# Splitting each layer's token tile into halves, with the second half's input projections placed beside (mLSTM/HGRN) or behind (SSD) the chunk recurrences of the first

## The chip, the cores and the metric

The kernel runs on all 8 cores of one Trainium2 chip. Every core executes the same program on its own share of the batch. The metric is the device time of the slowest core, in microseconds (us).

A program on 8 cores shows two states here. In the slow one the cores of one die, or of both, are granted a lower TensorE clock, and the time is some per cent longer (in one run of the kernel before, the cores of one die took 11202 to 11253 us at a clock of 0.723 to 0.729, those of the other 11531 to 11618 us at 0.688 to 0.695). Each execution is marked fast or slow by its cores' spans and clocks. Engines are named PE (TensorE matmul), PEld (TensorE weight load), DVE (VectorE), ACT (ScalarE), POOL and SP.

## The reference, cut to what matters

The program is one inference step of a two-layer trunk. One combined input projection feeds three head groups, each a recurrence over chunks of frames; an output projection and a feed-forward block (FFN) follow.

```python
def trunk_layer(x, state, p):
    h = rmsnorm(x, p['norm_mix'])
    proj = jnp.einsum('btd,dc->btc', h, p['w_in'])          # 1024 -> 6680 columns
    (z, xbc, dt_raw, mq, mk, mv, mi, mf, mo, hq, hf, hi, hgate) = split_cols(proj, IN_SIZES)
    conv = p['conv_b'] + sum(xpad[:, w:w + t] * p['conv_w'][w] for w in range(CONV_W))   # 4 taps, causal
    xbc = silu(conv)
    h_fin, y = lax.scan(ssd_chunk, h0, ssd_in)              # recurrence 1: SSD
    ...                                                     # gated by silu(z), rmsnorm
    (mc, mn, mm), hc = lax.scan(mlstm_chunk, carry0, ml_in) # recurrence 2: mLSTM
    y_ml = sigmoid(mo) * hc
    fgate = lb + (1 - lb) * sigmoid(hf)
    s_fin, o = lax.scan(gla_chunk, hg_st, hg_in)            # recurrence 3: HGRN2, log(fgate), silu(hq)
    y_hg = o * silu(hgate)
    x = x + einsum(concat([y_ssd, y_ml, y_hg]), p['w_out'])
    return x + swiglu_ffn(rmsnorm(x))                       # and the new states
```

The batch is 16 prompt streams of 2048 frames and 32 running streams of 32 frames. A core has 2 prompt streams, cut into tiles of 512 frames, and one sample tile of 4 streams of 32 frames. So it goes through 16 prompt layers (8 tiles, 2 layers) and 2 sample layers.

## The kernel before

The kernel records every operation with the keys it reads and writes, and a scheduler puts in the semaphores. Each engine's operations stand in its queue in the order in which the code commits them, and the trace shows PE taking its matmuls in that order: below, a projection that needs nothing from the chunks starts only 0.38 us after the start of their last matmul. A fence is one small DVE operation that comes after all work recorded before it and before all work recorded later. A prompt layer works through four chunks of 128 frames, in this order (cuts marked with dots):

```python
def layer(l, tile):
    ...
    fence_all()
    rmsnorm_fm(...)
    wvz, wkeyz = wload(w_in_v[:, :, 0:1024], 8, 1024, ...)       # a 2 MB slice of w_in
    ...
    def conv_chunk(b, cc):                  # one block of 128 channels, 512 frames
        ...
        V("act", copy(xp3[:, :, 3:3 + ls], PS[b][:, 0:n]))       # PSUM -> xp, ONE buffer
        ...
        V("dve", tensor_scalar(acc3, xp3[:, :, 0:ls], ...))      # tap 0, ONE accumulator cacc
        for w in range(1, 4):
            V("dve", scalar_tensor_tensor(acc3, xp3[:, :, w:w + ls], ...))
        V("act", activation(xbcT[:, cc, 0:n], cacc[:, 0:n], AF.Silu))
    for cc in range(12):
        b = fm_proj(wv, wkey, cc * 128, 128, n, hT, "hT", 8)     # 8 matmuls of 512 columns
        conv_chunk(b, cc)                                        # with z evictions in between
    ...
    pipelined([S.capture(one_chunk, l, tile, ci, ch, "ssd", ssd_chunk) for ci, ch in enumerate(chunks)], l)

    fence_all()
    ...                                                          # q, k, v, i, f: 512 columns each
    for ci, ... in enumerate(chunks):
        V("act", activation(oTM[...], PS[b], AF.Sigmoid))
    for hh in range(4):
        V("act", activation(gqT[:, hh, 0:n], PS[b], AF.Silu))
    for hh in range(4):                                          # the HGRN gate
        V("act", activation(cacc, PS[b], AF.Sigmoid))
        V("dve", tensor_scalar(cacc, cacc, oml, lb, ALU.mult, ALU.add))
        V("act", activation(gT[:, hh, 0:n], cacc, AF.Ln))
    ...
    for ci, ch in enumerate(chunks):                             # a "pair": same 128 frames
        la = S.capture(one_chunk, l, tile, ci, ch, "ml", mlstm_chunk)
        lb = S.capture(one_chunk, l, tile, ci, ch, "hg", hgrn_chunk)
        interleave2(la, lb)
```

`pipelined` puts the part of chunk c+1 that needs no carried state between the operations of chunk c. `interleave2(a, b)` cuts two lists of operations at their matmuls and deals them into the queues in turn. In the chunk loops two streams use four of the eight PSUM banks each.

## Time and profile before

| | before |
|---|---|
| time, median of the first 6 executions | 11292.55 us (11228.0 to 11406.7) |
| time, median of 20, beside the changed kernel | 11367.15 us (11228.0 to 11625.88) |

These lines of the page give the span, busy time by engine (share of the span, instructions), the DMA total and the chain of waits that ended last.

```profile
span 11256.1 us, 108345 instructions; the slowest of 8 cores (11192.9 to 11256.1 us)
PE 6586.1 (59%) x33519; PEld 3287.3 (29%) x33519; DVE 4136.5 (37%) x8286; ACT 3364.1 (30%) x6579; POOL 13.8 (0%) x37
...
DMA packets 596050, 766.59 MB, mean 68 GB/s; under 512 B 8884, under 2 KB 400332, under 8 KB 593160
...
PE 46%; DVE 18%; ACT 13%; issue 10%; DMA 8%; another core or an unknown queue 4%; DVEq 1%; ACTq 0%; SPq 0%
```

No engine is near full: PE 59%, DVE 37%, ACT 30%. The chain goes back and forth between engines, so the limits have to be looked for stage by stage. The windows view below shows one prompt layer, cut where its parts start. Columns: the stretch, its length, busy time and instruction count of PE, PEld, DVE, ACT and POOL, the granted clock, the DMA share and the rate. The rows are: norm, conv and SSD projections; SSD chunks; mLSTM/HGRN projections; pair one; pair two; pairs three and four with the output projection; FFN.

```profile
core 1: us, PE busy (x) PEld busy (x) DVE busy (x) ACT busy (x) POOL busy (x), PEclk, DMA share, GB/s
4828.13:4912.82 84.69, 44.72 (x176) 18.35 (x176) 42.31 (x83) 28.34 (x40) 0.00 (x0) 0.78 0.18 63
4912.82:5034.14 121.32, 69.72 (x364) 37.59 (x364) 62.64 (x94) 43.53 (x96) 0.00 (x0) 0.50 0.00 1
5034.14:5114.03 79.89, 67.21 (x296) 29.29 (x297) 6.48 (x20) 32.44 (x44) 0.00 (x0) 0.90 0.33 112
5114.03:5151.79 37.76, 12.33 (x81) 7.53 (x79) 21.93 (x53) 22.26 (x48) 0.00 (x0) 0.56 0.00 1
5151.79:5183.58 31.79, 10.38 (x72) 6.82 (x72) 21.82 (x53) 14.06 (x36) 0.00 (x0) 0.50 0.00 0
5183.58:5291.83 108.25, 50.83 (x273) 26.70 (x273) 49.94 (x116) 28.04 (x72) 0.00 (x0) 0.62 0.19 64
5291.83:5428.75 136.92, 121.64 (x548) 54.20 (x548) 28.60 (x44) 19.26 (x26) 1.47 (x5) 0.95 0.36 112
```

The first row is 84.69 us with PE busy for 44.72: not PE-bound. Its cause shows in the timeline of one conv block (start, length, engine, operation, what it waited for):

```profile
4864.30 0.72 ACT L143 ACTIVATE arenaB<-arenaB,arenaA 128x512 bf16<-128x512 f32 x1 [3.32 <-DVE arenaB L143]
...
4864.93 0.58 ACT L143 ACTIVATE arenaB<-ps 128x512 bf16<-128x512 f32 x1
4865.41 0.57 ACT L143 COPY arenaB<-ps 128x512 f32<-128x512 f32 x1
...
4866.16 0.48 DVE L143 TENSOR_SCALAR arenaB<-arenaB,arenaA 128x512 f32<-128x512 f32 x1
4866.75 2.46 DVE L143 SCALAR_TENSOR_TENSOR arenaB<-arenaB,arenaA 128x512 f32<-128x512 f32 x3
4869.30 0.72 ACT L143 ACTIVATE arenaB<-arenaB,arenaA 128x512 bf16<-128x512 f32 x1 [3.32 <-DVE arenaB L143]
```

The blocks follow each other every 5.0 us (4864.30 to 4869.30): Silu of the last block, a z eviction (the Silu that takes a block of z out of PSUM, the buffers that matmuls write), the copy into `xp`, four taps on DVE, Silu. With one `xp` and one `cacc` this is a single chain, and PE does not set its pace: it is busy through all of this block and for 0.48 us of the 5.0 us from 4874.30, where it waits for a weight load, and the chain's next round takes 5.06 us all the same (Silu at 4874.36 and at 4879.42).

The second row is a chain of latencies too (clock 0.50, nobody over 60% busy). In the third row PE is busy for 67.21 of 79.89 us at clock 0.90: after a wait of 10 us for the first weights, this one is PE's. Pairs run at clock 0.50 to 0.56 with PE busy for a third: here there is room for PE work, which is what the change aims at.

One line of the groups (count, busy us, mean ns):

```profile
L143 ACT ACT_TABLE_LOAD x291 | 373.4, 1283 | 642.1 <-PE ps L143 331.0
```

ACT loads a function table 291 times at 1283 ns.

To compare kernels, I took from the trace's start times the same marks in all 16 prompt layers and give medians: start of the layer, first scan (TENSOR_TENSOR_SCAN on DVE) of the SSD chunks, the state's cast in each of them, the second fence, the first scan of each pair, the third fence. All "steps" and "stages" below are worked out in this way, on the slowest core unless said otherwise.

### The profile page before, as it was taken

What the parts mean: (1) busy time and instruction counts of PE and PEld (TensorE: products, weight loads), DVE (VectorE), ACT (ScalarE), POOL (GpSimd) and SP (SyncE); (2) the same over time, 40 slices, a digit from 0 to 9 for tenths busy, and PEclk for the clock granted to TensorE, in tenths of its full rate; (3) what the DMA queues carried; (4) which work ended last, traced back from release to release, by engine and by line L of the source; (5) the groups of instructions that cost most, each with busy time, mean ns of one, the idle gap of its engine ahead of it and who ended that gap; (6) DMA issues with size and microseconds to landing.
All of it is one profiled execution on the core that took longest, in us unless ns stands there. A gap on an engine that the chain in (4) does not pass through costs nothing.

```text
span 11256.1 us, 108345 instructions; the slowest of 8 cores (11192.9 to 11256.1 us)
## 1 busy us (share of the span) xinstructions
PE 6586.1 (59%) x33519; PEld 3287.3 (29%) x33519; DVE 4136.5 (37%) x8286; ACT 3364.1 (30%) x6579; POOL 13.8 (0%) x37
## 2 busy tenths in 40 slices
PE   0046757575757566565657565757575665655444
PEld 0012323232323232222323232323232322223333
DVE  0033343434243433443343434342434334433333
ACT  0024242414242423323242424242424233231323
POOL 0000000000000000000000000000000000000000
PEclk9957767686868676767767676868686767676666
DMA  9941212121212121111212131212121211112323
GB/s 109 114 66 57 70 49 92 34 92 34 98 43 77 49 74 55 62 49 66 77 49 77 42 99 34 92 34 95 46 77 49 75 53 64 48 66 70 107 67 113
DMA packets 596050, 766.59 MB, mean 68 GB/s; under 512 B 8884, under 2 KB 400332, under 8 KB 593160
## 3 DMA queue, kind: packets, MB, share of 16 engines
q1 hardware_dynamic: 593032, 689.31, 18.7%
q0 software_dynamic: 2464, 70.35, 5.6%
q8 instruction: 291, 4.77, 0.2%
q14 instruction: 263, 2.15, 0.1%
HBM read 799.86 MB, written 100.48 MB: 80 GB/s over the span
## 4 chain that ended last, share of the span: by engine, by line
PE 46%; DVE 18%; ACT 13%; issue 10%; DMA 8%; another core or an unknown queue 4%; DVEq 1%; ACTq 0%; SPq 0%
PE ps L143 46%; DVE arenaB L143 15%; ACT arenaB L143 9%; DVE arenaA L143 3%; DMA arenaA<-w_in_b 2%; ACT arenaA L143 2%; ACT L143 1%; DMA arenaB<-x_prompt 1%; DVEq L139 1%; DMA arenaA<-w_ffn_out_b 1%; DMA arenaA<-w_out_b 0%; DMA arenaA<-w_ffn_in_b 0%; ACTq L139 0%; DMA arenaA<-conv_b 0%
## 5 line engine op out<-in xcount | busy, mean ns | idle before, releaser
L143 PE MATMUL ps<-arenaA 128*128 128x512 bf16 (+7 forms) x18051 | 4034.3, 385 | 1214.8 <-DMA arenaA<-norm_ffn 304.2
L143 PEld LDWEIGHTS ps<-arenaA 128*128 128x128 bf16 (+6 forms) x18051 | 1799.7, 104 | 3569.1 <-issue 1935.8
L143 PE MATMUL ps<-arenaA,arenaB 128*128 128x128 f32 (+14 forms) x4836 | 1156.9, 373 | 2156.3 <-ACT arenaB L143 945.7
L143 DVE TENSOR_TENSOR arenaB<-arenaB 128x512 f32<-128x512 f32 (+17 forms) x2184 | 1367.2, 643 | 913.6 <-ACT arenaB L143 825.7
L143 PE MATMUL ps<-arenaB,arenaA 128*128 128x512 bf16 (+6 forms) x6696 | 1225.3, 347 | 505.1 <-DVE arenaB L143 258.1
L143 PEld LDWEIGHTS ps<-arenaA,arenaB 128*128 128x128 f32 (+11 forms) x4836 | 592.8, 161 | 2376.8 <-issue 2359.6
L143 ACT ACTIVATE arenaB<-ps 128x512 bf16<-128x512 f32 (+6 forms) x1476 | 784.4, 532 | 1371.2 <-PE ps L143 1252.5
L143 ACT ACTIVATE arenaB<-arenaB 128x512 f32<-128x512 f32 (+15 forms) x1668 | 748.7, 454 | 1285.5 <-DVE arenaB L143 1233.4
L143 PEld LDWEIGHTS ps<-arenaB,arenaA 128*128 128x128 bf16 (+5 forms) x6696 | 685.0, 125 | 1088.7 <-issue 779.9
L143 PE MATMUL ps<-arenaB 128*128 128x64 bf16 (+8 forms) x3936 | 492.3, 264 | 788.3 <-DVE arenaB L143 648.7
L143 DVE TENSOR_TENSOR arenaA<-arenaA,ps 128x512 f32<-128x512 f32 (+2 forms) x648 | 394.6, 609 | 1410.0 <-PE ps L143 1396.4
L143 ACT ACTIVATE arenaB<-arenaA 128x4096 bf16<-128x4096 f32 (+1 forms) x45 | 149.9, 3332 | 2321.0 <-DVE arenaA L143 2321.0
L143 DVE TENSOR_TENSOR arenaB<-arenaB,ps 128x512 bf16<-128x512 bf16 (+5 forms) x684 | 414.1, 605 | 1153.6 <-PE ps L143 1114.0
L143 ACT ACT_TABLE_LOAD x291 | 373.4, 1283 | 642.1 <-PE ps L143 331.0
L143 PEld LDWEIGHTS ps<-arenaB 128*128 128x128 bf16 (+3 forms) x3936 | 292.5, 123 | 928.5 <-issue 916.9
L143 ACT ACTIVATE arenaA<-ps,arenaA 128x128 bf16<-128x128 f32 (+1 forms) x1152 | 414.2, 360 | 316.5 <-PE ps L143 233.3
L143 DVE SCALAR_TENSOR_TENSOR arenaB<-arenaB,arenaA 128x512 f32<-128x512 f32 (+1 forms) x648 | 457.9, 707 | 69.3 <-DVE arenaB L143 2.3
L143 ACT COPY arenaB<-ps 128x512 f32<-128x512 f32 (+9 forms) x648 | 359.6, 563 | 410.0 <-PE ps L143 393.4
L143 ACT ACTIVATE arenaB<-arenaB,arenaA 128x512 bf16<-128x512 f32 (+3 forms) x360 | 197.4, 548 | 868.9 <-DVE arenaB L143 862.2
L143 DVE SCALAR_TENSOR_TENSOR arenaA<-arenaA 128x512 bf16<-128x512 f32 (+3 forms) x360 | 254.4, 707 | 433.4 <-ACT arenaA L143 399.5
L143 DVE TENSOR_SCALAR arenaB<-arenaB,arenaA 128x512 f32<-128x512 f32 (+2 forms) x306 | 144.7, 473 | 529.6 <-ACT arenaB L143 529.4
L143 DVE COPY arenaA<-ps 128x512 f32<-128x512 f32 (+4 forms) x99 | 59.7, 603 | 618.6 <-PE ps L143 608.4
(37 smaller groups left out, 1702.5 us busy)
## 6 DMA issues: line engine op xcount, KB each, us to landing
arenaA<-w_in_b SPq DMA_DIRECT2D x90, 2048.0 KB
arenaA<-w_ffn_in_b SPq DMA_DIRECT2D x90, 2048.0 KB
arenaA<-w_ffn_out_b SPq DMA_DIRECT2D x72, 1408.0 KB
arenaA<-w_out_b SPq DMA_DIRECT2D x36, 2048.0 KB
w_in_b<-w_in POOLq DMA_DIRECT2D x2, 13360.0 KB, 290.9
w_ffn_in_b<-w_ffn_in POOLq DMA_DIRECT2D x2, 11264.0 KB, 435.9
arenaA<-w_in_b SPq DMA_DIRECT2D x18, 1056.0 KB
arenaA<-w_in_b SPq DMA_DIRECT2D x18, 1040.0 KB
```

What stands on the lines that cost most here:

```text
L139: eng.wait_ge(sem, val)
L143: ins = getattr(eng, name)(*a, **k)
```

## The change: intent and diff

The intent: cut each layer's tile in two halves of two chunks; run the projections of the second half on idle PE time while the chunk recurrences of the first half go on. It does so for both parts of the layer, but a switch (`DBGSEQ=True`) makes the SSD part sequential. For this the PSUM banks are divided into three, three and two, and the body of the SSD chunk takes its banks one group at a time.

```diff
-            i = 4 * p + (psk[p] % 4)
+            if p == 2:                       # the projections of the second half
+                i = 6 + (psk[2] % 2)
+                psk[2] += 1
+                return i
+            i = 3 * p + (psk[p] % 3)
...
+            hsplit = (len(allc) + 1) // 2 if len(allc) >= 2 else len(allc)
+            for part in (allc[:hsplit], allc[hsplit:]):
+                ...                          # t0, nt: first frame and length of the half
-            b = fm_proj(wv, wkey, cc * 128, 128, n, hT, "hT", 8)
+            def proj_ssd(sub):               # the same code for one half: weights loaded again,
+                ...                          # 256 columns, conv in two pieces
+                    b = fm_proj(wv, wkey, cc * 128, 128, nt, hT, "hT", 8, t0)
+            def proj_mlhg(sub):
+                ...
-            pipelined([S.capture(...) for ci, ch in enumerate(chunks)], l)
+            proj_ssd(subs[0])
+            for k, sub in enumerate(subs):
+                lists = [S.capture(one_chunk, l, tile, ci, ch, "ssd", ssd_chunk) for ci, ch in sub["chunks"]]
+                Y = S.capture(pipelined, lists, l)
+                if k + 1 < len(subs):
+                    X = cap_pool2(proj_ssd, subs[k + 1])
+                    if DBGSEQ:
+                        commit_all(Y)
+                        commit_all(X)
+                    else:
+                        interleave2(Y, X)
+                else:
+                    commit_all(Y)
...
+            proj_mlhg(subs[0])
+            for k, sub in enumerate(subs):
+                ...                          # Y: the pairs of this half, each interleaved as before
+                if k + 1 < len(subs):
+                    X = cap_pool2(proj_mlhg, subs[k + 1])
+                    interleave2(Y, X)
```

The sample tile is cut in the same way (its four streams of 32 frames become two and two).

## The prediction

> **What bounds the kernel now.** No single engine: busy times (page part 1) are PE 59%, DVE 37%, ACT 30%; the chain of waits runs 46% through PE, 18% DVE, 13% ACT. A prompt layer takes about 590 us; I cut one (timeline, 4832 to 5428 us) into stages with the windows view:
> - SSD projections and conv, 4845 to 4909: serial ACT-DVE-ACT chain, 5.03 us per 128-channel block with a z eviction, 4.55 us without; PE is not the limit.
> - SSD chunks, 4909 to 5034: PE 54% busy, DVE 51%, ACT 36%, clock 0.50. A latency chain: prologue 16.6 us, then 28.1 us per chunk, last body 18 us.
> - mLSTM/HGRN projections, 5044 to 5121: PE 69 of the first 72 us, clock 0.96.
> - mLSTM/HGRN chunks, 5121 to 5250: about 31.8 us per pair, DVE 60%, ACT 43%, PE 29%, clock 0.51.
> - output projection and FFN: PE-bound; untouched.
>
> **What the change does.** It hides half of the third stage in the first half of the fourth, where PE idles. In the SSD part it hides nothing: the switch is left at sequential, so second-half projections queue behind the first two chunks on every engine.
>
> **Costs per prompt layer** (estimates from trace durations):
> 1. Conv twice at 256 columns. The sample tile at 128 columns takes 3.0/2.5 us per block; interpolating, 3.67/3.2 at 256, so 40 us per half, 80 against 58: +22.
> 2. SSD pipeline broken in two: 2 x (16.6+28.1+18) against 16.6+3x28.1+18: +6.5. Handover +1.
> 3. Three PSUM banks instead of four per stream: +2 to +5.
> 4. First-half mLSTM/HGRN projections: PE 36 us, but 8.2 MB of weights are loaded again per half, and a 2 MB load takes about 9.6 us (issue 5076.9, PE resumes 5086.5), so DMA stretches it; with ACT's gate chain about 50, against 77: -27.
> 5. First two pairs, now with the second half's projections: 64 us alone. In-order queues insert 28 matmul groups, 28 evictions and some 20 extra table loads of 1.28 us (Sigmoid and Silu alternate with Exp; 13 today, all outside the chunk loop). Only two banks serve them. [...] I expect 105: +41.
> 6. Last two pairs unchanged.
>
> Sum about +45 per layer at worst; with a better overlap in 5 (85 us) +25. I take +35: 16 x 35 + 2 x 30 for the sample tile = +620, shaded to +590. Items 1, 2, 4, 5 lie on the critical path. W_in traffic doubles (+246 MB), mostly hidden.
>
> **Predicted:** 11880 us, range 11520 to 12260. Chances: faster by over 2% 0.06, within 2% 0.11, slower by over 2% 0.83.
>
> **What would show it.** DMA bytes about 1010 MB; table loads up from 291 to 600-800; conv period 3.2 to 3.7 us with PE idle; a second prologue in each SSD stage; no projection matmul before the last matmul of the first two SSD chunks; pairs one and two 45 to 60 us each, three and four about 32; FFN the same 118 us.
>
> **What would make it wrong.** [...] the inserted work fits the gaps (pairs near 40 us): about 11600. Key-level dependences and two banks serialise the streams: over 12200. If the SSD half had been interleaved after all, item 2 would turn to a gain.

No term of the sum is cut: +22, +6.5 and +1, +2 to +5, -27 and +41 make 45.5 to 48.5, recorded as about +45. The +41 was the author's estimate: the trace has a granted clock of 0.51 in the pairs against 0.96 in the dense projections, and the inserted matmuls might cost near double.

## The result, and the profile after

| | before | after |
|---|---|---|
| median | 11367.15 us (20 executions) | 12202.7 us (10 executions, 12102.09 to 12340.9) |
| ratio of fast runs | | 1.0766, 95% interval 1.0711 to 1.0822: slower |

A ratio is the mean time of one kernel's fast runs over that of the other's of the same rounds, so it is not quite the ratio of the medians above. The outputs are correct. The prediction had the class right, and 12202.7 lies within its range, but near its upper end.

The page of the changed kernel, the same lines as before:

```profile
span 12244.3 us, 124454 instructions; the slowest of 8 cores (12201.4 to 12244.3 us)
PE 7028.5 (57%) x37983; PEld 3783.5 (31%) x37983; DVE 4407.9 (36%) x9762; ACT 3971.1 (32%) x7821; POOL 13.8 (0%) x37
...
DMA packets 745896, 1013.88 MB, mean 83 GB/s; under 512 B 11188, under 2 KB 457932, under 8 KB 742920
...
PE 43%; DVE 18%; ACT 15%; issue 11%; DMA 8%; another core or an unknown queue 3%; DVEq 1%; ACTq 0%; SPq 0%
...
L146 ACT ACT_TABLE_LOAD x651 | 835.2, 1283 | 839.1 <-PE ps L146 491.7
```

The span of the profiled execution grew by 988 us (11256.1 to 12244.3). PE, DVE and ACT work grew by 442, 271 and 607 us. ACT's share of the chain rose from 13% to 15% and the waits for DMA stayed at 8%. Two predicted marks are there: 1013.88 MB against about 1010, and 651 table loads against 600 to 800.

The same layer in windows. The rows: norm and first-half conv; first two SSD chunks; second-half conv; last two SSD chunks; first-half mLSTM/HGRN projections; pair one; pair two; pairs three and four with the output projection; FFN.

```profile
core 7: us, PE busy (x) PEld busy (x) DVE busy (x) ACT busy (x) POOL busy (x), PEclk, DMA share, GB/s
5259.83:5324.10 64.27, 24.23 (x144) 14.69 (x144) 30.87 (x84) 20.84 (x36) 0.00 (x0) 0.72 0.42 148
5324.10:5387.40 63.30, 33.77 (x178) 18.34 (x179) 30.04 (x45) 20.94 (x45) 0.00 (x0) 0.50 0.00 1
5387.40:5434.80 47.40, 25.82 (x137) 14.51 (x135) 25.50 (x74) 15.81 (x35) 0.00 (x0) 0.72 0.07 23
5434.80:5502.45 67.65, 36.13 (x186) 19.80 (x186) 32.06 (x48) 22.04 (x48) 0.00 (x0) 0.50 0.00 1
5502.45:5561.94 59.49, 38.14 (x235) 23.96 (x236) 5.14 (x17) 24.03 (x38) 0.00 (x0) 0.82 0.61 204
5561.94:5603.00 41.06, 28.39 (x188) 17.02 (x186) 22.46 (x56) 26.43 (x60) 0.00 (x0) 0.80 0.22 75
5603.00:5659.56 56.56, 29.97 (x170) 17.42 (x168) 24.16 (x61) 42.10 (x70) 0.00 (x0) 0.64 0.11 40
5659.56:5768.81 109.25, 51.90 (x278) 26.78 (x276) 49.94 (x115) 30.00 (x74) 0.00 (x0) 0.64 0.19 63
5768.81:5906.75 137.94, 121.51 (x548) 54.11 (x548) 28.59 (x43) 19.27 (x26) 1.47 (x5) 0.95 0.35 111
```

Compare with before. Conv and projections of the SSD part took 84.69 us and now take 64.27 and 47.40. The chunks took 121.32 and now take 63.30 and 67.65. The mLSTM/HGRN projections fell from 79.89 to 59.49, pair one rose from 37.76 to 41.06, pair two from 31.79 to 56.56. The rest, with the FFN, is about the same here. In medians over all 16 prompt layers:

| step, us | before | after |
|---|---|---|
| layer start to first SSD scan | 84.7 | 63.7 |
| first scan to first chunk's state cast | 16.8 | 17.6 |
| chunk 1 to 2 | 28.2 | 28.4 |
| chunk 2 to 3 | 28.1 | 81.9 |
| chunk 3 to 4 | 28.2 | 28.4 |
| chunk 4 to fence | 17.4 | 18.6 |
| fence to pair one (projections) | 67.6 | 48.5 |
| pair one | 38.2 | 42.1 |
| pair two | 32.0 | 56.2 |
| pair three | 32.0 | 33.1 |
| **SSD stage** | **203.5** | **239.0** |
| **mLSTM/HGRN stage, with output projection** | **231.5** | **244.2** |
| **FFN stage** | **135.3** | **137.8** |

Adding the profiled layers up (sums, not medians): the SSD stages of the prompt layers grew by 565 us, the mLSTM/HGRN stages by 179, the two sample layers by 142 in all, and the FFN by 104. These make 990 of the 988 us.

The 104 us of the FFN come with a lower granted clock and not with more work; whether the change provokes that clock is left open. Two FFN stages of the changed kernel, of equal instruction counts in PE:

```profile
3781.90:3935.50 153.60, 138.91 (x536) 57.42 (x536) 26.66 (x41) 19.27 (x26) 0.00 (x0) 0.83 0.35 113
6424.50:6559.20 134.70, 119.78 (x536) 53.05 (x536) 26.64 (x40) 19.28 (x26) 0.00 (x0) 0.95 0.41 129
```

At a granted clock of 0.83 it takes 153.6 us, at 0.95 it takes 134.7. The clock records of the two traces hold only three values, 0.5, 0.8125 and 1, and the first of these stages spends 106.8 us at 0.8125, the second none. What sets the 0.8125, no run here shows. On the slowest core, the kernel before spends 251 us in all at 0.8125, the changed one 1091, the run e4 below none, and the other runs 1010 to 3122 (the FFN median of a profiled run lies at 135 to 138 us or at 157 to 158). Of the 1091 us, 721 lie in the FFN stages, 78 in pairs one and two, and none between the first SSD scan and the second fence. So I compare stages of the recurrences and leave the FFN out.

Now the two places where the time went. First the SSD part. The conv step in the changed kernel:

```profile
5283.30 0.51 ACT L146 ACTIVATE arenaB<-arenaB,arenaA 128x256 bf16<-128x256 f32 x1
5283.72 0.58 ACT L146 ACTIVATE arenaB<-ps 128x512 bf16<-128x512 f32 x1
5284.19 0.36 ACT L146 COPY arenaB<-ps 128x256 f32<-128x256 f32 x1
...
5284.74 0.34 DVE L146 TENSOR_SCALAR arenaB<-arenaB,arenaA 128x256 f32<-128x256 f32 x1
5285.19 1.66 DVE L146 SCALAR_TENSOR_TENSOR arenaB<-arenaB,arenaA 128x256 f32<-128x256 f32 x3
...
5287.00 0.51 ACT L146 ACTIVATE arenaB<-arenaB,arenaA 128x256 bf16<-128x256 f32 x1 [2.44 <-DVE arenaB L146]
```

A block of half the columns takes 3.7 us (5283.30 to 5287.00) where the whole block took 5.0: with half the columns the instructions take more than half the time. The copy went from 0.57 to 0.36 us, three taps from 2.46 to 1.66, Silu from 0.72 to 0.51. And nothing of it is hidden; this is where the second half's projections start, 0.38 us after the start of the second chunk's last matmul:

```profile
5387.19 0.59 PE L146 MATMUL ps<-arenaB 128*128 128x512 bf16 x1 [0.82 <-ACT arenaA L146]
...
5387.57 1.27 PE L146 MATMUL ps<-arenaA 128*128 128x256 bf16 x5
```

Second, pair two. ACT's timeline shortly after its start:

```profile
5604.89 1.28 ACT L146 ACT_TABLE_LOAD   x1 [0.24 <-DVE arenaB L146]
5606.18 0.40 ACT L146 ACTIVATE arenaB<-arenaB,arenaA 4x128 f32<-4x128 f32 x1
5606.60 1.28 ACT L146 ACT_TABLE_LOAD   x1
5607.90 0.38 ACT L146 ACTIVATE arenaB<-ps 128x256 bf16<-128x256 f32 x1
5608.30 1.28 ACT L146 ACT_TABLE_LOAD   x1
5609.59 0.80 ACT L146 ACTIVATE arenaB<-arenaB 4x128 f32<-4x128 f32 x2
...
```

The 128x256 evictions are Silus of the inserted projections, the 4x128 operations are mLSTM's exponentials. A load stands between the one function and the other, the queue alternates between them, and every turn takes ACT 1.28 us. Nothing more is seen: after each of the 651 loads the next activation starts 11 to 12 ns after the load's end. There are 16 loads in this step of every prompt layer, before there was none. ACT, busy for 14.06 us of pair two before, is now busy for 42.10.

### The profile page after: what moved, and what is told of

The parts are those of the page before. It is cut to its first block, busy times and chain, and to the rows that moved or that the text cites. A ratio compares the mean times of both kernels' runs of the same rounds, so it can differ in the third digit from the quotient of the medians.

```text
span 12244.3 us, 124454 instructions; the slowest of 8 cores (12201.4 to 12244.3 us)
## 1 busy us (share of the span) xinstructions
PE 7028.5 (57%) x37983; PEld 3783.5 (31%) x37983; DVE 4407.9 (36%) x9762; ACT 3971.1 (32%) x7821; POOL 13.8 (0%) x37
## 2 busy tenths in 40 slices
DMA packets 745896, 1013.88 MB, mean 83 GB/s; under 512 B 11188, under 2 KB 457932, under 8 KB 742920
## 4 chain that ended last, share of the span: by engine, by line
PE 43%; DVE 18%; ACT 15%; issue 11%; DMA 8%; another core or an unknown queue 3%; DVEq 1%; ACTq 0%; SPq 0%
PE ps L146 43%; DVE arenaB L146 15%; ACT arenaB L146 10%; DVE arenaA L146 3%; ACT L146 3%; DMA arenaA<-w_in_b 3%; ACT arenaA L146 2%; DVEq L142 1%; DMA arenaB<-x_prompt 1%; DMA arenaA<-w_out_b 1%; ACTq L142 0%; DMA arenaA<-w_ffn_out_b 0%; DMA arenaA<-w_ffn_in_b 0%; DMA arenaA<-ml_gain 0%
## 5 line engine op out<-in xcount | busy, mean ns | idle before, releaser
L146 PE MATMUL ps<-arenaA 128*128 128x512 bf16 (+7 forms) x22515 | 4547.8, 366 | 1831.4 <-ACT arenaB L146 531.1
L146 PEld LDWEIGHTS ps<-arenaA 128*128 128x128 bf16 (+4 forms) x22515 | 2320.7, 110 | 4047.5 <-issue 2878.0
L146 PE MATMUL ps<-arenaA,arenaB 128*128 128x128 f32 (+14 forms) x4836 | 1116.5, 363 | 2348.6 <-ACT arenaB L146 1146.1
L146 ACT ACTIVATE arenaB<-ps 128x512 bf16<-128x512 f32 (+8 forms) x1692 | 819.5, 485 | 1351.6 <-PE ps L146 1246.2
L146 ACT ACTIVATE arenaB<-arenaB 128x4 f32<-128x4 f32 (+12 forms) x1776 | 765.4, 438 | 1202.6 <-DVE arenaB L146 1149.4
L146 PE MATMUL ps<-arenaB 128*128 128x128 bf16 (+8 forms) x3936 | 478.7, 256 | 564.7 <-DVE arenaB L146 440.1
L146 DVE SCALAR_TENSOR_TENSOR arenaB<-arenaB,arenaA 128x256 f32<-128x256 f32 (+1 forms) x1296 | 598.7, 462 | 137.7 <-DVE arenaB L146 3.2
L146 ACT ACTIVATE arenaB<-arenaB,arenaA 128x256 bf16<-128x256 f32 (+3 forms) x576 | 260.9, 453 | 1026.3 <-DVE arenaB L146 1020.6
L146 ACT COPY arenaB<-ps 128x256 f32<-128x256 f32 (+8 forms) x864 | 388.6, 460 | 466.0 <-PE ps L146 443.5
L146 ACT ACTIVATE arenaA<-ps,arenaA 128x128 bf16<-128x128 f32 (+1 forms) x1152 | 412.7, 358 | 310.3 <-PE ps L146 229.7
L146 DVE TENSOR_SCALAR arenaB<-arenaB,arenaA 128x256 f32<-128x256 f32 (+3 forms) x612 | 214.4, 350 | 648.1 <-ACT arenaB L146 647.0
```

Source lines behind the costliest of these rows:

```text
L146: ins = getattr(eng, name)(*a, **k)
```

## The experiments

Theory T: the SSD part pays for a second conv pass, a second pipeline start and fewer banks, and hides nothing. The mLSTM/HGRN part does hide work, but the cut itself makes the projections dearer by more than is hidden, and most of what is lost there is table loads. Rivals: the doubled weight traffic; the PSUM banks; PE's granted clock, 0.50 to 0.56 in the pairs before; or that interleaving hides nothing at all.

Runs of one batch were made on the same chip. The chip of the first batch (e1 to e4) gave the kernel before 11326.9 to 11620.04 us and nearly only slow runs, the second batch (e5 to e8) one slow run of 11646.05. Whole times there are therefore of little use at the scale of a per cent, and I give the steps of the trace. Where the profiled execution was slow, I checked the steps on the core with the highest clock (0.70 to 0.73); the chunk and pair steps differ by about 3 us at most from core to core (pair one of the changed kernel: 42.0 to 45.0); its FFN stages differ more (medians of 136.0 to 144.0 us across its cores).

### e1: the SSD half of the change alone

```diff
-            subs = ...                  # halves for both parts
+            subs = cut(halves)          # SSD part
...
+            subs = cut((allc,))         # mLSTM/HGRN part whole
```

> Only the SSD part is cut in halves; the mLSTM/HGRN part is whole again (three-bank pools kept). Theory (each half pays its own serial costs): nearly all of the SSD cost stays, +35 us per prompt layer and +41 per sample layer, so about 11290+650 = 11940 us, ratio to before near 1.058; the mLSTM/HGRN stage is back at about 232 us per layer. Rival (the doubled weight traffic is what slows everything): the SSD half carries 5.2 of the 13.4 MB that are loaded again, so only 39% of the loss, ratio near 1.03.

Measured: median 12064.59 us of 4 runs; the two fast ones 11957.56 and 12006.39, against the only fast run of before on this chip, 11326.9 (ratio 1.058, as T expected; the rival's 1.03 is out). SSD stage 238.9 us (239.0 with the whole change); pairs one and two back at 38.2 and 32.0 us. So the SSD part is about +35 us a prompt layer by itself, and the larger share of the loss.

### e2: the mLSTM/HGRN half alone

```diff
+            subs = cut((allc,))         # SSD part whole
...
+            subs = cut(halves)          # mLSTM/HGRN part
```

> Only the mLSTM/HGRN part is cut in halves. Theory: +10 us per prompt layer and +35 per sample layer, plus up to 40 us of FFN drift: ratio near 1.02 to 1.03, pairs 42, 56, 33, 31 us as in the changed kernel, SSD stage back at about 204 us. Rival (weight traffic): this part carries 8.2 of 13.4 MB, so 61% of the loss, ratio near 1.047.

Measured: median 11820.1 us of 6 runs, the only fast one 11544.59, 1.9% over the only fast run of before (11326.9), where the rival expected 4.7%. SSD stage 205.7 us. The mLSTM/HGRN stage is 241.8 us on the undisturbed core of highest clock (231.1 on before's), 244.1 on the slowest; pair two is 56.2 us with its 16 table loads. So this half also loses, by 11 to 13 us a layer: what it takes out in front (67.6 to 48.2) it gives back in the pairs.

### e3: no split, but the new PSUM banks and SSD body

```diff
+            subs = cut((allc,))         # both parts whole; banks 3 + 3 + 2 stay
```

> Nothing is cut; only the three-bank pools and the per-group order of the SSD body remain of the change. Theory: about +2 to +5 us per prompt layer (the second group's matmul now waits for a bank), ratio 1.003 to 1.008, SSD chunk period 28.4 instead of 28.1 us. Rival: banks were slack, ratio 1.000.

Measured: median 11528.22 us of 6 runs. SSD stage 206.7 us, +3 (the first body 17.6 against 16.8, the end 18.6 against 17.4); pairs unchanged at 38.1 and 32.1. The banks as the main cause are out: they are 3 of 35 us. Whole times would mislead here: the four fast runs (11478.56 to 11578.85) lie 1.3 to 2.2% above the one fast run of before, and 3 us a layer are 0.5%; the profiled one has an FFN median of 156.9 us, at the lower clock.

### e4: the SSD half interleaved, as the switch allows

```diff
-def build(NPS, TP, NSS, dbg=False, LAG=8, DBGSEQ=True):
+def build(NPS, TP, NSS, dbg=False, LAG=8, DBGSEQ=False):
```

> The changed kernel with the SSD switch set to interleave. Theory of the prediction (item 2 would turn to a gain): the 36 us of second-half conv hide partly in the first two chunks, total about 11650 us. Rival that I now think likelier: conv brings 29 us of DVE and 16 Silu evictions among Exps into a chunk stage that is a latency chain on the same ACT and DVE queues, with 20 to 30 more table loads per layer; then the gain is small or none, 12000 to 12250 us.

Measured: median 12150.8 us of 5 runs, fast ones 11966.37 and 12027.65. The SSD stage is 228.8 us: 10 less than in the changed kernel, still 25 more than before. The first two chunks together with the second half's conv, the windows view of the same layer:

```profile
5125.11:5225.20 100.09, 55.71 (x311) 30.18 (x309) 53.13 (x119) 59.32 (x98) 0.00 (x0) 0.64 0.04 12
```

That is 100.09 us where the changed kernel takes 63.30 + 47.40 = 110.70. Work is hidden, but ACT is now busy for 59.32 us of it, with 22 table loads in the SSD stage where there were 5 (the conv's Silu alternates with the chunks' exponentials). My prediction had said that interleaving here would turn the item into a gain. It does not; it makes the loss smaller. What it would do without the switches was not run.

### e5: the conv and projections in two halves, the chunks in one pipeline

```diff
-            proj_ssd(subs[0])
-            for k, sub in enumerate(subs): ...
+            for sub in subs:
+                proj_ssd(sub)
+            pipelined([S.capture(one_chunk, l, tile, ci, ch, "ssd", ssd_chunk) for ci, ch in allc], l)
...
+            subs = cut((allc,))         # mLSTM/HGRN part whole
```

> SSD projections and conv run in two halves one after the other, then all four chunks as one pipeline; mLSTM/HGRN whole. Theory: only the halved conv is paid, +22 us per prompt layer (layer start to first scan 85 to about 107 us), chunk periods stay 28.3 us, SSD stage median near 228 us against 206.7 of the banks-only kernel. Rival (the broken pipeline and the handover are most of the +35): stage near 212 us.

Measured (two executions, the profiled one of 12103.06 us slow; steps of the undisturbed core): layer start to first SSD scan 108.8 us against 84.6, so +24.2. The chunk steps stay at 28.3. The conv in two pieces is the largest single term of the SSD loss.

### e6: the conv whole, the chunks in two pipelines

```diff
+            proj_ssd(cut((allc,))[0])
+            for sub in cut(halves):
+                pipelined([S.capture(one_chunk, l, tile, ci, ch, "ssd", ssd_chunk) for ci, ch in sub["chunks"]], l)
```

> SSD projections whole; the four chunks run as two pipelines of two. Theory: the second prologue and the first tail are exposed, so the step from the second to the third chunk grows from 28.3 to about 36 us (18.6 tail + 17.6 prologue), SSD stage median near 214 us; with e5 the two parts add up to the 239 us of the changed kernel within 5 us, because the sequential order hides nothing. Rival: they add up to clearly more than 239, so something was hidden after all.

Measured (one look, 11533.72 us): chunk 2 to 3 takes 35.85 us against 28.3, +7.5; SSD stage 213.1. With e3 and e5: 203.5 + 3.2 (banks) + 24.2 (conv twice) + 7.5 (second pipeline) = 238.4, and the changed kernel has 239.0. The SSD loss is accounted for, within 1 us by these steps and within 2.4 by the stages' medians (206.7 in e3, 230.2 in e5, 213.1 here).

### e7: sigmoid and silu of the mLSTM/HGRN projections made of Exp and Ln

```diff
-    V("act", activation(gqT[:, hh, ts], PS[b], AF.Silu))
+    V("act", activation(cacc, PS[b], AF.Exp, scale=-1.0))       # e^-x
+    V("act", activation(cacc, cacc, AF.Ln, bias=1.0))           # ln(1 + e^-x)
+    V("act", activation(cacc, cacc, AF.Exp, scale=-1.0))        # sigmoid(x)
+    V("dve", tensor_tensor(gqT[:, hh, ts], cacc, PS[b], ALU.mult))
```

> The changed kernel with Sigmoid and Silu of the mLSTM/HGRN projections computed by Exp, Ln, Exp from the table that the chunks use (result unchanged up to rounding). Theory (table loads are most of what the hidden half costs): the 16 loads in the second pair vanish, 16 x 1.28 = 20 us, so pair two falls from 56 to about 38 to 42 us although ACT gets 24 more short instructions; pair one stays at 42; the first-half projections also lose 10 loads, 48 to about 43 us. Rival (in-order PE queue, two banks, slow clock make the cost): pair two stays above 50 us.

Measured (two executions, 12063.75 and 12194.09 us; steps of the undisturbed core): the table loads fall to 111; pair two falls from 56.2 to 45 us; the mLSTM/HGRN stage is 230.0 us (244.2 in the changed kernel, 231.1 before). Two expectations were missed: pair two was to fall to 38 to 42 us, and the first-half projections, which were to fall to 43, rose to 53.4. No load stands in pair two any more, so changing between Exp and Ln takes none there. Three instructions now do one's work, so this run takes away 20 us of loads and adds 24 ACT instructions. That is why e9 follows.

### e8: the slices of `w_in` not loaded in full, in both halves

Wrong result: after the first loads, only one eighth of each slice of `w_in` is fetched.

```diff
-            S.dma("sp", v, src3, [wbkey], ["w%d" % i])
+            if wbkey.startswith("wb_in") and wk[0] > 60:
+                S.dma("sp", v[:, 0:1, :], src3[:, 0:1, :], [wbkey], ["w%d" % i])
+            else:
+                S.dma("sp", v, src3, [wbkey], ["w%d" % i])
```

> The changed kernel with an eighth of every W_in load after the first tile (wrong result on purpose). Theory: weight traffic costs only the wait in the first-half mLSTM/HGRN projections, about 6 us of their 48; SSD stage (239) and pairs (42, 56, 33, 31) unchanged within 1 us. Rival (doubled traffic slows the engines' work in general): SSD stage and the pairs fall by several us each, FFN too.

Measured (slow runs only; steps of the undisturbed die, cores 4 to 7, against the same cores of the changed kernel): the first-half mLSTM/HGRN projections fall from 47.8 to 48.8 us down to 41.2 to 42.0, and the stage from 243.1 to 244.2 us down to 234.1 to 236.8 (e4, with the same mLSTM/HGRN part and a higher clock, has 241.5 to 243.5); pair two stays at 56, the SSD steps do not move. In the sample layers the SSD stage falls from 229.5 to 215.5 us and the mLSTM/HGRN stage from 235.5 to 213. So the traffic of `w_in` is worth 5 to 8 us of a prompt layer and about 36 of a sample layer. These are upper bounds for the second loading: the run thins the first loading too, which the kernel before also pays for, and the kernel before was not run with thin weights. In a prompt layer the weights are thus at most 8 of the 48 us lost, in a sample layer at most half.

### e9: each sigmoid and silu replaced by one instruction without a table switch

Its output is wrong, which doesn't matter for the time. It separates the loads from e7's extra instructions.

```diff
-    V("act", activation(gqT[:, hh, ts], PS[b], AF.Silu))
+    V("act", activation(gqT[:, hh, ts], PS[b], AF.Identity, scale=0.5))    # same for o and the output gate
-    V("act", activation(cacc, PS[b], AF.Sigmoid))
+    V("act", activation(cacc, PS[b], AF.Exp, scale=-0.05))
```

> Wrong result on purpose: the changed kernel, with the Sigmoid and Silu of the mLSTM/HGRN projections replaced by one instruction each from the table in use. Theory (the 16 table loads of 1.28 us in pair two are 20 us): the step from pair two to pair three falls from 56 us to 36-40; the 45 us that the run with exponentials left was its extra ACT instructions. What stays over 32 us is work in order on PE and ACT. The step of pair one stays near 38-42. Rival (PE work at the low clock and two banks cost the step, not the tables): it stays at 45 or over.

Measured (11865.9 us): pair two 39.8 us, within the 36 to 40 that T expected; the rival's 45 is out. Pair one is 44.4, a little over. Pair two in the windows view:

```profile
5280.07:5319.73 39.66, 26.63 (x170) 16.13 (x169) 23.90 (x61) 19.89 (x52) 0.00 (x0) 0.74 0.15 54
```

ACT is busy for 19.89 us of pair two, against 42.10 in the changed kernel; PE has the same 170 matmuls. The 16.4 us between 56.2 and 39.8 are what the switches cost in pair two (16 loads of 1.28 us are 20.5, so a part of them was hidden). In the first-half projections, 10 loads fewer go with 41.5 us instead of 48.5; from the fence to pair three, 29 loads fewer go with 20.9 us less. What remains over 32.0 is 7.8 us.

### e10: the second half's mLSTM/HGRN projections after the pairs, not between them

```diff
-                    interleave2(Y, X)
+                    commit_all(Y)
+                    commit_all(X)
```

> The changed kernel with the second-half mLSTM/HGRN projections queued whole after the first two pairs instead of between their chunks. Theory: pair one 38 us, pair two 32 plus about 45 us of projections, so the mLSTM/HGRN stage goes from 244 to about 261 us a prompt layer: interleaving does hide some 14-17 us, which is less than the split and its table loads cost. Rival (interleaving hides nothing): the stage stays at 244 or falls.

Measured (one run; its clocks of 0.683 to 0.702 are among the lowest here): 12815.94 us; stage 267.6 us. Pair one, and pair two with the second-half projections behind it, in the windows view:

```profile
5736.73:5772.81 36.08, 10.41 (x72) 6.83 (x72) 21.91 (x54) 20.11 (x44) 0.00 (x0) 0.50 0.00 1
5772.81:5851.74 78.93, 44.91 (x271) 28.11 (x276) 25.03 (x65) 38.11 (x74) 0.00 (x0) 0.71 0.19 67
```

Pair one is back to what it was, with 10.41 us of PE. This run splits the account. From the fence to the start of pair three and of pair four, in medians over the prompt layers:

| from the fence, us | to pair three | to pair four |
|---|---|---|
| before | 137.5 | 169.7 |
| halves, in sequence (e10) | 167.0 | 204.4 |
| halves, interleaved (the change) | 146.9 | 180.2 |
| interleaved, one instruction without switch (e9, wrong result) | 126.0 | 158.2 |

The sums to pair four are the ones to use for e10: its pair three takes 38.0 us (33.1 in the changed kernel), and part of the second-half projections lies in it (93 matmuls start in this step of the layer shown, against 75). The cut alone costs 34.7 us. The projections took 67.6 us whole; in halves they take 50.1 and at least 79.6 - 32.0 = 47.6. Interleaving takes 24.2 back, more than the 14 to 17 that I expected, and the rival "hides nothing" is out. With no switches in the queue it would have been a gain of 11.5 over before. From core to core these sums differ by 1 to 5 us, and the core shown is the lowest of the changed kernel's (180.2 to 182.9) and the highest of e9's (155.2 to 158.2).

### e11: the kernel before with its gates grouped by table

```diff
     for hh in range(4):
+        V("act", activation(gT[:, hh, 0:n], PS[b], AF.Sigmoid))     # right after o's sigmoid
+        ...
     for hh in range(4):
         V("act", activation(gqT[:, hh, 0:n], PS[b], AF.Silu))
-    for hh in range(4):
-        ...                                                         # Sigmoid, DVE, Ln, four times
     ...
+    V("act", activation(gT[:, :, 0:n], gT[:, :, 0:n], AF.Ln))       # one, 2048 wide
```

> The kernel before, reordered only: gate sigmoids directly after o's sigmoid, then the silus, then one logarithm 2048 wide: 3 table loads instead of 12 a layer. Theory: 9 loads of 1.28 us are 11.5 us of ACT, but PE bounds this stretch, so only 4-8 us a layer come off the time: ratio 0.990-0.995. Rival (ACT is wholly hidden there): 1.00.

```profile
L143 ACT ACT_TABLE_LOAD x129 | 165.5, 1283 | 520.4 <-PE ps L143 277.7
```

Measured: 162 loads fewer, 9 a layer as planned, and no time: median 11530.31 us of 4 runs against 11431.19 of 7; the one fast run has 11522.14, the two fast ones of before 11429.58 and 11442.16. From the fence to the start of pair two, on the core with the highest clock of each run, it takes 106.4 us, and 105.3 before. My expectation of 4 to 8 us a layer was a miss: in this stretch PE is the limit and ACT's loads are wholly hidden. A load that costs about 1 us in pair two (16.4 us over 16) costs nothing here.

### e12: only the mLSTM/HGRN part of prompt tiles cut, and no switching in the pairs

SSD whole with its old banks and body; sample tile whole; first-half gates grouped as in e11; the interleaved half with Exp and Ln as in e7. The result is correct.

```diff
+            if p >= 4:                               # SSD: four banks a stream again
+                i = 4 * (p - 4) + (psk[p] % 4)
+            subs = cut(halves if tile["kind"] == "p" else (allc,))
-                    X = cap_pool2(proj_mlhg, subs[k + 1])
+                    X = cap_pool2(proj_mlhg_1t, subs[k + 1])    # e7's functions
```

> SSD whole as before; mLSTM/HGRN in halves for prompt tiles only, first-half gates grouped, second half interleaved with sigmoid and silu made of Exp and Ln, which need no table switch. Theory: the mLSTM/HGRN stage takes 224-228 us against 231 before, so ratio 0.99-1.00, and no better than the reordering alone. Rival (overlap pays once the table loads are gone): 215 us or less, ratio 0.98 or less.

The windows view of first-half projections, pair one and pair two:

```profile
4937.55:4980.20 42.65, 28.35 (x187) 19.20 (x190) 5.15 (x17) 11.57 (x23) 0.00 (x0) 0.83 0.62 211
4980.20:5027.22 47.02, 37.25 (x258) 22.66 (x258) 22.75 (x57) 31.18 (x74) 0.00 (x0) 0.96 0.55 180
5027.22:5072.06 44.84, 24.88 (x142) 14.65 (x144) 26.31 (x67) 25.43 (x66) 0.00 (x0) 0.66 0.00 1
```

Measured: 11153.74, 11258.21 (fast), 11291.96, 11347.42 (slow); before, in the same rounds: 11429.58, 11442.16 (fast) and five slow ones from 11385.35. The ratio of fast runs is 11205.98 / 11435.87 = 0.980, of two runs each, too few for an interval; but each of the four runs is faster than each of the seven. ACT is busy for 25.43 us of pair two, with 66 instructions and no load. (Pair one's first scan does not wait for the last gates in this kernel, so its start is not the end of the projections; I compare sums only.) From the fence to pair three it takes 131.3 us, 6.2 less than before; over the whole stage the mean is 229.7 us a prompt layer against 237.8, which is 16 x 8.1 = 130 us or 1.2% of the time. The stage's median, 226.2 us, is within the 224 to 228 expected; that it would be no better than the reordering alone was wrong. (The profiled span, 11256.4 us, equals that of before: its FFN stages took 125 us more, with 1824 us at the clock of 0.8125 instead of 251.) So there is a gain of 1 to 2% in this idea, and e11 shows that it does not come from the regrouping.

## Why the prediction was right, point by point

It was right in class, and its steps were seen one by one. Its size was low: +590 us predicted, 836 between the medians (11367.15 and 12202.7), 988 in the profiled executions. One announced mark was missed: pair one, at 42.1 us, stayed below 45 to 60.

1. **"Conv twice at 256 columns ... +22."** Measured +24.2 (e5). The period of 3.7 us with a z eviction was predicted at 3.67.
2. **"SSD pipeline broken in two ... +6.5. Handover +1."** Measured +7.5 (e6). No projection matmul starts before the last matmul of the second chunk, as said.
3. **"Three PSUM banks ... +2 to +5."** Measured +3.2 (e3). With 1 and 2 the SSD part was to be about +33 and is +35.5.
4. **"First-half mLSTM/HGRN projections ... about 50, against 77: -27."** The 50 was right (48.5 with interleaving, 50.1 without). The 77 was not: I had read it in one layer, and that layer is one of four with a long third row (77.5 to 79.9 us, with the 10 us of waiting for weights; the median of 16 is 67.6). The gain is -19.
5. **"First two pairs ... I expect 105: +41."** Measured 98.3 us. The base is 38.2 + 32.0 = 70.2 rather than 64, since pair one is longer than the others, so +28. The mechanism is as said: the loads alternate (16 in pair two, 16.4 us by e9). The estimate that inserted matmuls may cost near double was too dark: with the inserted work the granted clock was 0.80 in pair one and 0.64 in pair two of the layers shown, where it was 0.56 and 0.50 before, and 0.50 in pair one of e10, without inserted work. Items 4 and 5 sum to +14 predicted, +9.4 measured (146.9 against 137.5); their errors cancel, which is luck.
6. **"Last two pairs unchanged."** Nearly: pair three takes 33.1 us (32.0 before), and from pair four to the third fence it is 63.7 (62.0).

**What was mis-sized.** The items sum to +45, and the stages measured +35.5 and +12.7, so +48. I then took +35, leaning to "a better overlap in 5 (85 us)", which no run shows: that is 16 x (46.5 - 35) = 184 us with the mean growth of 46.5 (565 and 179 over 16). The last shading, from +620 to +590, is another 30. The sample tile was put at "2 x 30"; its stages grew by 41 and 35 us in each layer, about 76, so 92 more: with 128 columns in all it waits for weights, which are loaded twice (e8 takes back 36 of the 76, an upper bound). The FFN's 104 us of lower clock were not foreseen; they differ from run to run. 590 + 184 + 30 + 92 + 104 = 1000, and 988 were measured (the FFN of the two sample layers was 10 us shorter).

**"If the SSD half had been interleaved after all, item 2 would turn to a gain."** Wrong: e4 has 228.8 us, a smaller loss. Item 1 stays in full, and 22 table loads come in.

What stays open: what decides in which layers the die's clock is lowered, and whether the changed kernel provokes that more often than the one before. What a second loading of the weights costs apart from the first, and what an interleaved SSD half would give without switches, were not run. The 7.8 us that pair two keeps over its old 32 in e9 were not taken apart into PE's order, the two banks and ACT's evictions.

## What to carry to other kernels

Before cutting a tile to overlap its halves, measure what the halves cost in sequence: here two half projections took 98 us where the whole took 68, so an overlap that hid 24 us was a loss. Before putting two streams into one ACT queue, count the table loads that their functions take; loads that cost nothing here in a PE-bound stretch (9 a layer fewer: 106.4 against 105.3 us, e11) cost most of their time inside a latency chain (16.4 of 20.5 us, e9). And take a stage's base from all layers, not from the one that happened to be open in the trace.
